# Gates and branch products computed with tokens on the partitions, and latents scaled by 1/rms before they are transposed

## The chip, the cores and the metric

One core of a Trainium2 chip runs the whole program. Its engines are TensorE (PE, matrix products; PEld is its loading of the stationary operand), VectorE (DVE), ScalarE (ACT), GpSimd (POOL) and SyncE (SP, which issues the weight transfers). The metric is the device time of one execution in microseconds.

## The reference

A trunk of two layers works on 256 tokens of width 1024, all in float32. Each layer is a gated feed-forward block, a mixer and a second feed-forward block. The change lies in the mixer:

```python
h = rms_norm(x, mix_norm[l])
rg_x, rg_g, sb_q, sb_k, sb_v, c_q, c_kv, k_r, gate_logits = split(h @ w_in[l])
y_a = rg_lru(conv(rg_x)) * gelu(rg_g)                 # recurrence
y_b = stick_breaking_attention(sb_q, sb_k, sb_v)      # 8 heads
y_c = mla_branch(c_q, c_kv, k_r, ...)                 # rms_norm(c_q) @ w_uq, rms_norm(c_kv) @ w_ukv, softmax attention
g_a, g_b, g_c = split(sigmoid(gate_logits))
merged = g_a * (y_a @ w_branch_a) + g_b * (y_b @ w_branch_b) + g_c * (y_c @ w_branch_c)
x = x + merged @ w_out[l]
```

The three gates and the three branch products are 1024 x 1024 products for 256 tokens each. `c_q` and `c_kv` (the latents) are 256 wide.

## The kernel before

**Products in three parts.** Each float32 weight is split into a high and a low part: ACT casts a piece of 1024 columns to `hi`, and DVE subtracts to get `lo`. Activations are split in the same way into `r` tiles that hold high and low part side by side. A product is hi x hi + hi x lo + lo x hi.

**Two kinds of group.** A *feature group* makes 256 output features on the partitions and keeps tokens along the columns. For each 128 rows of the input (a k-step) the weight is the stationary operand: two matmuls of 512 columns with `hi` (the activations' two parts at once), then two of 256 columns with `lo`. In a view these read `acc<-r,hi` and `acc<-r,lo`. The two halves of the 512 columns are added afterwards (`features`: an ACT copy and a DVE add), and a column of 1/rms values has to be spread over the partitions first (`broadcast`, a matmul against a constant) to be multiplied in. A *token group* makes 512 output features along the columns with the tokens on the partitions. For each k-step the activations are stationary, and each half of the tokens takes three matmuls of 512 columns: `acc<-hi,r`, `acc<-lo,r`, `acc<-hi,r`. Its result is complete, and 1/rms is one number per partition.

**Order.** `MIX_ORDER` is a list, written by hand, of the mixer's groups; `v0` is a token group, `q0` a feature group, and so on. The weights lie in memory in that order and arrive in it. All other work of a layer (the recurrence, two attentions, norms, transposes) is written as tasks. After each k-step `Tasks.tick` lets the tasks add instructions to the engines' queues, by a planner that keeps its own estimates of when each engine is free (`Clock`, `Op.cost`, `fits`). The order is fixed when the program is built; each engine then runs its queue strictly in order. Where a group needs a result that a task has not yet issued, `tasks.drain` issues the rest of that task at once.

**Buffers.** PSUM has two `acc` buffers of two banks, used in turn by groups, and four `side` banks for tasks and for short or last groups (`small_banks`). The dependencies are tracked by tile, so an instruction that reads one half of a tile waits for the writer of the other half too.

**The steps that the change touches.** `latents` copies a latent out of PSUM, transposes it with four 128 x 128 transposes (`side<-cst,f`), splits it with `hilo`, and only then squares it, gets 1/rms on POOL and broadcasts it (`side<-f,cst`), for `head_T` to multiply in. `gate` scales a group and takes a tanh; `branch` multiplies a group by its gate and adds it to `merged`; the third branch of a feature block also splits the sum into an `r` tile, `mT`, which the groups `out0` to `out3` read. `rg_chain` is the recurrence, pair by pair of blocks (four pairs): it splits the block weights and the input into `r` tiles and multiplies them (`side<-r,r`). In the profile all recorded instructions have line L201, so they are told apart by their tiles.

Of the kernel before, what the change touches and what calls it, by code (L numbers as in the profile page):

```python
# [14 lines left out]
NT = S // 128  # L15
# [15 lines left out]
MIX_ORDER = tuple((x.rstrip("0123"), int(x[-1])) for x in """  # L31
v0 k0 rgx0 rgx1 k1 q0 q1 cq0 q2 q3 k2 rgx2 v1 k3 rgx3 rgg0 rgg1 rgg2 rgg3
gb0 uq0 gb1 uq1 gb2 uq2 gb3 uq3 uqr0 brb0 brb1 ckv0 brb2 brb3 ga0 ukv0 ga1 ukv1 uv0 ga2 ukv2
ga3 ukv3 bra0 bra1 uv1 gc0 bra2 gc1 gc2 gc3 brc0 brc1 brc2 brc3 bra3 out0 out1 out2 out3
""".split())
# [3 lines left out]
    "rgx": ("in", 0, KD), "rgg": ("in", 1024, KD), "q": ("in", 2048, KD), "k": ("in", 3072, KD), "cq": ("in", C_C, KD),  # L39
    "ga": ("in", C_G, KD), "gb": ("in", C_G + 1024, KD), "gc": ("in", C_G + 2048, KD),  # L40
    "uq": ("uq", 0, 2), "ukv": ("ukv", 0, 2), "bra": ("bra", 0, KD), "brb": ("brb", 0, KD), "brc": ("brc", 0, KD), "out": ("out", 0, KD),
    "dn1": ("dn1", 0, KF), "dn2": ("dn2", 0, KF),
}
TOKENS = {"last": ("dn2", 0, KF), "v": ("in", 4096, KD), "uqr": ("uq", 1024, 2), "uv": ("ukv", 1024, 2)}


def group_stream(what, n):

    if what == "ckv":
        for k in range(0, 9, 3):  # L50
            yield ("ckv0", "in", k, C_C + 256)
            yield ("ckv1", "in", k, C_C + 256)
    elif what in TOKENS:
# [284 lines left out]
def trunk(tc, xT_in, pos_in, w_in, rgw_in, fin_in, const_in, out):  # L338
# [4 lines left out]
    with ctx:  # L343
# [167 lines left out]
        def feature_group(kts, evac, last=0):  # L511
# [19 lines left out]
            return finish(evac, a, tasks.LAST if last else None)  # L531

        def plain_group(c, xg, evac, norm):

# [55 lines left out]
        def scaled(a, src, key, extra=None, plain=False):  # L590

            if plain:
# [6 lines left out]
                return f  # L599
            f = yield from features(a)  # L600
            while key not in src:
                yield 1
# [76 lines left out]

        def broadcast(b, r, dst, key, start=False):  # L680
# [4 lines left out]
            pe.matmul(b[:, 256:512], neg_one, d[:, 0:256], start=start, stop=True, skip_group_check=True)  # L685
# [131 lines left out]

        def gen_scaled(a, scales):

            o = []  # L820
            for t in range(NT):
                f = yield from FT.take()
                if t == 0:
# [118 lines left out]
        def head_T(mx, key, p, r, extra=None):  # L942

            def run(a):
                f = yield from scaled(a, mx["nm"] if r == "rb" else mx, r, extra)
                yield
                mx[key][p] = f
# [65 lines left out]
        def latents(mx, i):  # L1013
            def run(a):
# [16 lines left out]
                yield  # L1031
                side.give(b)
                mx["cT"][i] = hl
                yield
                junk = yield from FT.take()
                for t in range(NT):
                    act.activation(out=junk[:, 0:256], in_=cs_[t], func=AF.Square, accum_out=mx["ssc"][:, i, t:t + 1])
                yield
                FT.give(junk, c)
                rsqrt_mean(mx["rc"][:, i], mx["ssc"][:, i], 256)  # L1040
                yield
# [20 lines left out]
        def q_rope(mx):  # L1062
            def run(a):
                qs = yield from gen_scaled(a, mx["rq"])
                yield
# [125 lines left out]
        def mix(nm, ntasks, nxt, l):  # L1191
# [6 lines left out]
            mx["rc"] = pool.tile([128, 2, NT], F32, name=f"rc{l}")  # L1198
            mx["rq"] = [mx["rc"][:, 0, t:t + 1] for t in range(NT)]
            mx["rkv"] = [mx["rc"][:, 1, t:t + 1] for t in range(NT)]  # L1200
            mx["sm"] = pool.tile([128, 3, HEADS, NT], F32, name=f"sm{l}")
# [41 lines left out]
            def gate(b, n):  # L1243
                def sigmoid(f):

                    act.activation(out=f, in_=f, func=AF.Tanh, scale=0.5)
                    yield
                    sig[b, n] = f

                def run(a):  # L1250
                    f = yield from scaled(a, mx["nm"], "rb")
                    yield
                    tasks.spawn(sigmoid(f))
                return run

            def branch(i, b, n):

                def run(a):
                    f = yield from FT.take()
                    hl = (yield from RT.take()) if i == 2 else None  # L1260
                    while (b, n) not in sig or (i and n not in merged):
                        yield 1
                    s = sig.pop((b, n))
                    m = merged[n] if i else None
                    for c, ap in parts(a):
                        fc, sc = two(f)[:, c], two(s)[:, c]
                        act.copy(fc, ap[:, :, 256:512])
                        dve.tensor_tensor(fc, ap[:, :, 0:256], fc, op=ALU.add)
                        if type(a) is not list:
                            yield  # L1270
                            give_banks(a)
                        dve.scalar_tensor_tensor(out=fc, in0=sc, scalar=1.0, in1=fc, op0=ALU.add, op1=ALU.mult)
                        if i:
                            mc = two(m)[:, c]
                            dve.tensor_tensor(mc, mc, fc, op=ALU.add)
                        if i == 2:
                            act.copy(hl[:, c, 0], mc)
                            dve.tensor_tensor(hl[:, c, 1], mc, hl[:, c, 0].bitcast(F32), op=ALU.subtract)
                    yield
                    if type(a) is list:  # L1280
                        give_banks(a)
                    FT.give(s)
                    if i == 0:
                        merged[n] = f
                        return
                    FT.give(f)
                    if i == 2:
                        FT.give(m)
                        mT[n] = hl
                return run  # L1290
# [16 lines left out]
            for g in MIX_ORDER:  # L1307
# [5 lines left out]
                elif what == "uq":  # L1313
                    feature_group(Latent(0), head_T(mx, "qn", n, "rbq"))
                elif what == "uqr":
                    token_group(Latent(0), q_rope(mx))
                elif what == "ukv":
                    feature_group(Latent(1), head_T(mx, "kn", n, "rbkv"))
                elif what == "uv":
                    token_group(Latent(1), head_v(mx, "v_ml", n, mx["rkv"]))  # L1320
                elif what == "rgx":
# [7 lines left out]
                elif what in ys:  # L1329
                    mtask[n] = feature_group(Pairs(mx[ys[what]], lambda p: work[what][p:p + 1] if what == "bra" else work[what], KD), branch(turn[g], what[2], n), last=4 if g == branches[-1] else 0)  # L1330
                elif what == "out":
                    out_tasks.append(feature_group(Pairs(mT, lambda p: [mtask[p]], KD), lambda a, n=n: update_x(n, a, 0.5, nxt), last=4 if n == 3 else 0))
                else:
                    feature_group(kts, gate(what[1], n))
                if what in ys and n == 3:
                    RT.give(*mx[ys[what]].values())
# [3 lines left out]
                if g == last_of("rgx", "rgg", "q", "k", "v", "cq", "ckv", "ga", "gb", "gc"):  # L1340
                    RT.give(*nm["xT"].values())
            FT.give(nm["rb tile"], mx["rbq tile"], mx["rbkv tile"])
            FT.give(mx["kr"])
# [174 lines left out]
```

## Time and profile before

| | us |
|---|---|
| median of 3 runs | 1461.55 (1461.19 to 1462.02) |
| the profiled execution's own time | 1463.23 |
| its span, first to last instruction | 1461.4 |
| PE busy in the span | 1442.5 |
| DVE busy | 1108.8 |
| ACT busy | 888.8 |

The span is the part of the execution that the trace covers; 1.8 us lie around it. A busy time is the time in which an engine had at least one instruction under way. Matmuls overlap each other in the pipeline, so the cost of one is the distance from its start to the next one's start, not its duration.

### The profile page before, as it was taken

To read this page: it belongs to the slowest core of one execution; us is meant where nothing else is said; L and a number is where in the kernel's file an instruction comes from. 1 tells how busy PE (TensorE), PEld (TensorE's weight loads), DVE (VectorE), ACT (ScalarE), POOL (GpSimd) and SP (SyncE) were. 2 spreads that over 40 slices of the span, in tenths; PEclk is the share of its full clock that TensorE was granted. 3 is DMA by queue.
4 is the path that set the end of the run, shared out by engine and by line. 5 is a ranking of instruction groups with operands and counts; after the bars stand their busy time and mean duration, and the time that the engine had idled before them with its cause. 6 is when DMAs were issued, how large, how long until landed. Compare 5 with 4: busy or idle time off the path is not lost.

```text
span 1461.4 us, 20833 instructions
## 1 busy us (share of the span) xinstructions
PE 1442.5 (99%) x8276; PEld 1261.0 (86%) x8276; DVE 1108.8 (76%) x1548; ACT 888.8 (61%) x1365; POOL 144.5 (10%) x118
## 2 busy tenths in 40 slices
PE   8999999999999999999999999999999999999998
PEld 7888889888888888888888888898888888888886
DVE  5887567689987788876677776676989877877853
ACT  4665446888665556555455554479885656566543
POOL 2000001123410000000000000111323000100001
PEclk9999999999999999999999999999999999999999
DMA  6555554444543455455545455544444434545452
GB/s 244 201 185 192 200 179 163 170 151 147 197 148 145 171 179 194 179 200 178 198 173 201 177 198 184 200 159 155 141 171 174 173 138 166 199 175 201 176 199 87
DMA packets 37506, 258.17 MB, mean 177 GB/s; under 512 B 4256, under 2 KB 4640, under 8 KB 6816
## 3 DMA queue, kind: packets, MB, share of 16 engines
q1 hardware_dynamic: 35856, 253.16, 48.0%
q0 software_dynamic: 832, 2.62, 0.6%
q8 instruction: 65, 1.06, 0.3%
q10 hardware_dynamic: 720, 1.05, 0.2%
q14 instruction: 33, 0.27, 0.1%
HBM read 255.77 MB, written 1.05 MB: 176 GB/s over the span
## 4 chain that ended last, share of the span: by engine, by line
PE 90%; DVE 7%; issue 1%; ACT 1%; DMA 0%; ACTq 0%; POOLq 0%; POOL 0%; DVEq 0%
PE acc L201 76%; PE side L201 14%; DVE f L201 3%; DVE lo L201 3%; DVE r L201 1%; DMA x<-xT 0%; ACT f L201 0%; ACT hi L201 0%; ACT r L201 0%; ACTq L396 0%; POOLq L1514 0%; POOL rms L201 0%; DVE rms L201 0%; DVEq L201 0%
## 5 line engine op out<-in xcount | busy, mean ns | idle before, releaser
L201 PE MATMUL acc<-r,hi 128*128 128x512 f32 x3116 | 1000.3, 402 | 0.0
L201 DVE TENSOR_TENSOR lo<-raw,hi 128x1024 fp32r<-128x1024 f32 (+1 forms) x478 | 591.4, 1239 | 231.4 <-ACT hi L201 230.2
L201 PEld LDWEIGHTS acc<-r,lo 128*128 128x128 f32 x3116 | 585.2, 188 | 137.7
L201 PE MATMUL acc<-r,lo 128*128 128x256 f32 x3116 | 613.4, 278 | 0.0
L201 ACT CAST hi<-raw 128x1024 fp32r<-128x1024 f32 (+1 forms) x478 | 496.9, 1045 | 128.8 <-PE acc L201 91.9
L201 PEld LDWEIGHTS acc<-r,hi 128*128 128x128 f32 x3116 | 481.5, 189 | 5.0
L201 POOL TENSOR_TENSOR f<-f,f 128x512 f32<-128x512 f32 (+1 forms) x51 | 90.9, 1787 | 1043.3 <-ACT f L201 959.9
L201 ACT COPY f<-acc 128x512 f32<-128x512 f32 x164 | 96.0, 585 | 121.4 <-PE acc L201 121.2
L201 ACT ACTIVATE f<-f 128x256 f32<-128x256 f32 (+3 forms) x190 | 94.9, 502 | 85.6 <-DVE f L201 84.4
L201 DVE TENSOR_TENSOR f<-acc,f 128x512 f32<-128x512 f32 x166 | 113.9, 686 | 41.6 <-ACT f L201 41.2
L201 DVE TENSOR_TENSOR f<-f,f 128x512 f32<-128x512 f32 (+1 forms) x177 | 125.0, 706 | 7.8 <-ACT f L201 1.6
L201 ACT CAST r<-f 128x256 fp32r<-128x256 f32 (+2 forms) x130 | 58.7, 456 | 63.4 <-DVE f L201 59.7
L201 PE MATMUL acc<-hi,r 128*128 128x512 f32 (+2 forms) x344 | 96.9, 358 | 0.0
L201 PE MATMUL side<-r,hi 128*128 128x512 f32 x260 | 84.5, 396 | 0.0
L201 PE MATMUL side<-f,f 128*128 128x256 f32 (+1 forms) x320 | 71.7, 328 | 0.0
L201 PEld LDWEIGHTS acc<-hi,r 128*128 128x128 f32 x344 | 61.6, 189 | 8.3
L201 DVE TENSOR_TENSOR r<-f,r 128x256 fp32r<-128x256 f32 (+2 forms) x130 | 64.7, 502 | 1.9 <-ACT r L201 1.9
L201 PE MATMUL acc<-lo,r 128*128 128x512 f32 (+2 forms) x172 | 61.0, 355 | 0.0
L201 PE MATMUL side<-r,lo 128*128 128x256 f32 x260 | 60.5, 279 | 0.0
L201 PEld LDWEIGHTS side<-r,hi 128*128 128x128 f32 x260 | 45.6, 188 | 7.5
L201 PEld LDWEIGHTS side<-r,lo 128*128 128x128 f32 x260 | 47.0, 188 | 4.0
L201 PEld LDWEIGHTS side<-f,f 128*128 128x128 f32 x320 | 46.0, 191 | 0.5
(95 smaller groups left out, 839.1 us busy)
## 6 DMA issues: line engine op xcount, KB each, us to landing
raw<-w SPq DMA_DIRECT2D x239, 1024.0 KB, 4.8
f<-rgw POOLq DMA_DIRECT2D x8, 256.0 KB, 3.6
raw<-w SPq DMA_DIRECT2D x4, 256.0 KB, 5.7
out<-f SPq DMA_DIRECT2D x4, 256.0 KB, 2.2
x<-xT ACTq DMA_DIRECT2D x3, 256.0 KB, 6.9
f<-fin POOLq DMA_DIRECT2D x2, 256.0 KB, 3.4
cst<-const SPq DMA_DIRECT2D x1, 336.0 KB, 8.3
x<-xT ACTq DMA_DIRECT2D x2, 128.0 KB, 3.8
```

Of the source, the lines that this page charges most:

```text
L201: return self.f(*self.args, **self.kw)
```

## The change

The gates and branches become token groups: 12 groups of 256 features become 6 of 512 for each of the two kinds in a layer. `gate` now copies both token halves out with ACT, times 1/rms; `branch` multiplies straight out of PSUM. `merged` has tokens on the partitions, so after the last branch it is transposed (16 transposes a layer) before it is split into `mT`. The groups `out0` and `out1` become one `outs0`, which goes through the first half of the k-steps for both and then through the second half. The latents are squared first, multiplied by 1/rms on DVE and then transposed, so that four broadcasts go, and the heads need no scaling. `MIX_ORDER` is rewritten.

```diff
-v0 k0 rgx0 rgx1 k1 q0 q1 cq0 q2 q3 k2 rgx2 v1 k3 rgx3 rgg0 rgg1 rgg2 rgg3
-gb0 uq0 gb1 uq1 gb2 uq2 gb3 uq3 uqr0 brb0 brb1 ckv0 brb2 brb3 ga0 ukv0 ga1 ukv1 uv0 ga2 ukv2
-ga3 ukv3 bra0 bra1 uv1 gc0 bra2 gc1 gc2 gc3 brc0 brc1 brc2 brc3 bra3 out0 out1 out2 out3
+v0 k0 rgx0 rgx1 k1 q0 q1 cq0 q2 q3 k2 rgx2 v1 k3 rgx3 rgg0 rgg1 uq0 rgg2 uq1 rgg3 uq2
+gb0 uq3 gb1 uqr0 brb0 ckv0 brb1 ukv0 ga0 ukv1 uv0 ga1 ukv2 bra0 ukv3 uv1 gc0 gc1 bra1 brc0 brc1
+outs0 out2 out3
...
+        def feature_pair(kts, evacs):
+            nk = len(kts)
+            a = [bank() for _ in range(2)]
+            it = iter(kts)
+            for f in range(2):
+                half = [next(it) for _ in range(nk // 2)]
+                for n in range(2):
+                    for i, (h, _, hl) in enumerate(half, f * nk // 2):
...
@@ latents
+                junk = yield from FT.take()
+                for t in range(NT):
+                    act.activation(out=junk[:, 0:256], in_=cs_[t], func=AF.Square, accum_out=mx["ssc"][:, i, t:t + 1])
+                yield
+                FT.give(junk)
+                rsqrt_mean(mx["rc"][:, i], mx["ssc"][:, i], 256)
+                for t in range(NT):
+                    dve.tensor_scalar(cs_[t], cs_[t], mx["rc"][:, i, t:t + 1], None, op0=ALU.mult)
                 yield
                 b = yield from transpose_pair(cs_, 0)
...
-                b = yield from side.take()
-                yield from broadcast(b, mx["rc"][:, i], mx, ("rbq", "rbkv")[i], start=True)
@@ gate
-                    f = yield from scaled(a, mx["nm"], "rb")
+                    for t in range(NT):
+                        f = yield from FT.take()
+                        act.activation(out=f, in_=bank_of(a, t), func=AF.Copy, scale=mx["rcol"][t])
...
@@ branch
-                        act.copy(fc, ap[:, :, 256:512])
-                        dve.tensor_tensor(fc, ap[:, :, 0:256], fc, op=ALU.add)
...
-                        dve.scalar_tensor_tensor(out=fc, in0=sc, scalar=1.0, in1=fc, op0=ALU.add, op1=ALU.mult)
+                    for t, f in enumerate(fs):
+                        dve.scalar_tensor_tensor(out=f, in0=f, scalar=1.0, in1=bank_of(a, t), op0=ALU.add, op1=ALU.mult)
+                        if i:
+                            dve.tensor_tensor(merged[n][t], merged[n][t], f, op=ALU.add)
...
+                    if i == 2:
+                        for q in range(2):
+                            x = yield from transpose_pair(merged[n], q * 256)
+                            hl = yield from RT.take()
+                            hilo(x, hl)
```

**How the order moves.** Three places are shown. Tile names carry buffer numbers here; on PE the names behind the arrow are the moving and then the stationary operand.

*First place: the gates of branch b in layer 0, where `rg_chain` multiplies pairs 2 and 3.* Before, PE's queue at the start of `gb0` reads as follows (`r8`, `r7` belong to pair 2, `r3`, `r13` to pair 3).

```order
L201 MATMUL side2_88<-r3_93,r13_103 128x256 x4
L201 MATMUL acc0_84<-r15_105,hi_2946 128x512 x2
L201 MATMUL acc0_84<-r15_105,lo_2947 128x256 x2
L201 MATMUL side3_89<-r8_98,r7_97 128x256 x4
L201 MATMUL acc0_84<-r15_105,hi_2946 128x512 x2
L201 MATMUL acc0_84<-r15_105,lo_2947 128x256 x2
```

DVE's queue before, from the low part `lo_2947`, which the feature group reads just then, to the last split of pair 3.

```order
L201 TENSOR_TENSOR lo_2947<-raw_2811,hi_2946 128x1024
L201 TENSOR_TENSOR f17_123<-acc0_84,f17_123 128x512
L201 TENSOR_TENSOR f17_123<-f17_123,f2_108 128x512
L201 SCALAR_TENSOR_TENSOR f26_132<-f24_130,f25_131 128x256
L201 TENSOR_TENSOR r8_98<-f14_120,r8_98 128x512
L201 TENSOR_TENSOR lo_2980<-raw_2811,hi_2979 128x1024
L201 TENSOR_TENSOR r13_103<-f15_121,r13_103 128x512
L201 TENSOR_TENSOR r3_93<-f16_122,r3_93 128x512
```

In the changed order PE's queue in the sixth of `gb0`'s eight k-steps (pair 3 is now `r6`, `r13`).

```order
L208 MATMUL acc0_84<-hi_3058,r1_91 128x512
L208 MATMUL acc0_84<-lo_3059,r1_91 128x512
L208 MATMUL acc0_84<-hi_3058,r1_91 128x512 x2
L208 MATMUL acc0_84<-lo_3059,r1_91 128x512
L208 MATMUL acc0_84<-hi_3058,r1_91 128x512
L208 MATMUL side2_88<-r6_96,r13_103 128x256 x4
L208 MATMUL acc0_84<-hi_3091,r1_91 128x512
L208 MATMUL acc0_84<-lo_3092,r1_91 128x512
```

And DVE's queue from three rows ahead of that split.

```order
L208 SCALAR_TENSOR_TENSOR r11_101<-f8_114,r11_101 128x2x256
L208 TENSOR_TENSOR f34_140<-side3_89,f34_140 128x256
L208 TENSOR_TENSOR lo_3092<-raw_2966,hi_3091 128x1024
L208 TENSOR_TENSOR r6_96<-f28_134,r6_96 128x512
L208 TENSOR_TENSOR lo_3109<-raw_2966,hi_3108 128x1024
```

The four matmuls of pair 3 stood in front of a weight part (`lo_2947`) that DVE makes seven rows ahead of pair 3's own split; now their split comes one row behind the weight part that the next matmuls read (`lo_3092`). Pair 2's matmuls moved back into `rgg0`, where their split stands five rows behind the stream's weight part instead of seven.

*Second place: behind `ckv0`, the second latent.* Before, PE's queue in the feature group `brb3`: the broadcast (`f16`, the constant as stationary) ahead of the group's last k-step.

```order
L201 MATMUL acc0_84<-r4_94,hi_3536 128x512 x2
L201 MATMUL acc0_84<-r4_94,lo_3537 128x256 x2
L201 MATMUL side1_87<-f16_122,cst_72 128x256
L201 MATMUL acc0_84<-r4_94,hi_3536 128x512 x2
L201 MATMUL acc0_84<-r4_94,lo_3537 128x256 x2
```

In the changed order PE's queue in the token group `brb1`, between the halves of its sixth k-step: the transposes of the scaled latent (`f31`) and three of the queries' rope part.

```order
L208 MATMUL acc0_84<-hi_3451,r4_94 128x512 x2
L208 MATMUL acc0_84<-lo_3452,r4_94 128x512
L208 MATMUL acc0_84<-hi_3451,r4_94 128x512
L208 MATMUL side3_89<-cst_72,f31_137 128x128 x4
L208 MATMUL side2_88<-cst_72,f35_141 128x128
L208 MATMUL side2_88<-cst_72,f15_121 128x128
L208 MATMUL side2_88<-cst_72,f35_141 128x128
L208 MATMUL acc0_84<-hi_3451,r4_94 128x512
L208 MATMUL acc0_84<-lo_3452,r4_94 128x512
```

The broadcast is gone. The transposes that start the latent's split now wait for the squares, 1/rms and the scaling, and `ukv0`, which reads the split, starts at the end of this group.

*Third place: from the last branch group to the output groups.* Before, PE's queue from the last k-steps of `bra3` into `out0`; the `r` tiles that `out0` reads in its first six k-steps (`r15`, `r0`, `r1`) come from earlier branch groups.

```order
L201 MATMUL side3_89<-r4_94,hi_4793 128x512 x2
L201 MATMUL side3_89<-r10_100,hi_4793 128x512 x2
L201 MATMUL side3_89<-r4_94,lo_4794 128x256 x2
L201 MATMUL side3_89<-r10_100,lo_4794 128x256 x2
L201 MATMUL acc1_85<-r15_105,hi_4817 128x512 x2
L201 MATMUL acc1_85<-r15_105,lo_4818 128x256 x2
L201 MATMUL acc1_85<-r15_105,hi_4817 128x512 x2
L201 MATMUL acc1_85<-r15_105,lo_4818 128x256 x2
```

In the changed order PE's queue at the middle of `outs0`: `f16` and `f27` hold the two token halves of `merged` from `brc1`, `r7` is the first tile split from them.

```order
L208 MATMUL acc1_85<-r4_94,lo_4386 128x256 x2
L208 MATMUL side0_86<-cst_72,f16_122 128x128
L208 MATMUL acc1_85<-r4_94,hi_4385 128x512 x2
L208 MATMUL acc1_85<-r4_94,lo_4386 128x256 x2
L208 MATMUL side0_86<-cst_72,f27_133 128x128
L208 MATMUL side0_86<-cst_72,f16_122 128x128
L208 MATMUL side0_86<-cst_72,f27_133 128x128
L208 MATMUL side3_89<-cst_72,f16_122 128x128
L208 MATMUL side3_89<-cst_72,f27_133 128x128
L208 MATMUL side3_89<-cst_72,f16_122 128x128
L208 MATMUL side3_89<-cst_72,f27_133 128x128
L208 MATMUL acc0_84<-r7_97,hi_4422 128x512 x2
```

DVE's queue at the same place, from the low part of `r4` (the tile that the first half of `outs0` reads in its third and fourth k-step) on; `f4` and `f33` are `brc1` times its gate.

```order
L208 TENSOR_TENSOR r4_94<-side3_89,r4_94 128x2x256
L208 TENSOR_TENSOR lo_4423<-raw_4336,hi_4422 128x1024
L208 SCALAR_TENSOR_TENSOR f4_110<-f4_110,side2_88 128x512
L208 TENSOR_TENSOR f16_122<-f16_122,f4_110 128x512
L208 SCALAR_TENSOR_TENSOR f33_139<-f33_139,side1_87 128x512
L208 TENSOR_TENSOR f27_133<-f27_133,f33_139 128x512
L208 TENSOR_TENSOR lo_4447<-raw_4336,hi_4446 128x1024
L208 TENSOR_TENSOR r7_97<-side0_86,r7_97 128x2x256
L208 TENSOR_TENSOR r10_100<-side3_89,r10_100 128x2x256
```

The last branch's sum stands on DVE behind the split of `r4` and one weight part, and PE's transposes of it stand directly ahead of the matmuls that read their result.

## Rows read from the trace of the kernel before

**Rows 1.** The page: busy time, then TensorE's granted clock, then the ending chain.
```profile
PE 1442.5 (99%) x8276; PEld 1261.0 (86%) x8276; DVE 1108.8 (76%) x1548; ACT 888.8 (61%) x1365; POOL 144.5 (10%) x118
...
PEclk9999999999999999999999999999999999999999
...
PE 90%; DVE 7%; issue 1%; ACT 1%; DMA 0%; ACTq 0%; POOLq 0%; POOL 0%; DVEq 0%
```

**Rows 2.** The waits of PE over the whole span.
```profile
PE side L201 <- DVE r L201: 4.7, 4, 1.5
...
PE side L201 <- DVE f L201: 2.4, 4, 1.0
```

**Rows 3.** PE's timeline in a feature group: start, duration, operation, out<-moving,stationary.
```profile
211.28 0.63 PE L201 MATMUL acc<-r,hi 128*128 128x512 f32 x2
211.75 0.40 PE L201 MATMUL acc<-r,lo 128*128 128x256 f32 x2
...
214.07 0.62 PE L201 MATMUL acc<-r,hi 128*128 128x512 f32 x2
```

**Rows 4.** PE's timeline in a token group.
```profile
200.14 0.62 PE L201 MATMUL acc<-hi,r 128*128 128x512 f32 x2
...
205.58 0.61 PE L201 MATMUL acc<-hi,r 128*128 128x512 f32 x2
```

**Rows 5.** PE's timeline around four transposes of the first latents.
```profile
257.03 0.60 PE L201 MATMUL side<-cst,f 128*128 128x128 f32 x4
...
257.94 0.40 PE L201 MATMUL acc<-r,lo 128*128 128x256 f32 x2
```

**Rows 6.** PE's timeline around a broadcast that nothing holds up.
```profile
210.16 0.59 PE L201 MATMUL side<-f,cst 128*128 128x256 f32 x2
...
211.05 0.40 PE L201 MATMUL acc<-r,lo 128*128 128x256 f32 x2
```

**Rows 7.** PE's timeline around the broadcast of the second latents' 1/rms.
```profile
402.29 0.40 PE L201 MATMUL acc<-r,lo 128*128 128x256 f32 x2
403.73 0.70 PE L201 MATMUL side<-f,cst 128*128 128x256 f32 x2 [1.04 <-DVE f L201]
...
404.72 0.40 PE L201 MATMUL acc<-r,lo 128*128 128x256 f32 x2
```

**Rows 8.** PE's timeline at the transposes of the queries' rope part.
```profile
394.74 0.27 PE L201 MATMUL side<-cst,f 128*128 128x128 f32 x1
395.17 0.55 PE L201 MATMUL side<-cst,f 128*128 128x128 f32 x3 [0.16 <-DVE f L201]
```

**Rows 9.** PE's timeline at the recurrence blocks' matmuls of pairs 2 and 3.
```profile
335.23 0.36 PE L201 MATMUL side<-r,r 128*128 128x256 f32 x1
336.47 0.39 PE L201 MATMUL side<-r,r 128*128 128x256 f32 x1 [0.88 <-DVE r L201]
...
338.57 0.28 PE L201 MATMUL side<-r,r 128*128 128x256 f32 x1
340.31 0.62 PE L201 MATMUL side<-r,r 128*128 128x256 f32 x3 [1.46 <-DVE r L201]
```

**Rows 10.** DVE's timeline just before and in those waits.
```profile
336.34 1.63 DVE L201 TENSOR_TENSOR lo<-raw,hi 128x1024 fp32r<-128x1024 f32 x1
337.89 2.36 DVE L201 TENSOR_TENSOR r<-f,r 128x512 fp32r<-128x512 f32 x2
```

**Rows 11.** GpSimd's timeline in the same stretch.
```profile
336.98 2.13 POOL L201 TENSOR_TENSOR f<-f,f 128x512 f32<-128x512 f32 x1
```

**Rows 12.** ScalarE by form: the high half of a transposed block.
```profile
L201 ACT CAST r<-side 128x512 fp32r<-128x512 f32 x16 | 9.4, 586 | 17.3 <-PE side L201 17.2
```

**Rows 13.** VectorE by form: count, busy time, mean ns of one.
```profile
L201 DVE TENSOR_TENSOR lo<-raw,hi 128x1024 fp32r<-128x1024 f32 x474 | 588.3, 1242 | 229.7 <-ACT hi L201 228.4
...
L201 DVE SCALAR_TENSOR_TENSOR f<-f,f 128x512 f32<-128x512 f32 x46 | 32.6, 716 | 1.0
...
L201 DVE TENSOR_TENSOR r<-side,r 128x512 fp32r<-128x512 f32 x16 | 10.9, 683 | 5.1 <-ACT r L201 5.1
```

More of the change, by code (lines that the diff above doesn't have):

```diff
@@ L52, in group_stream @@
             yield ("ckv1", "in", k, C_C + 256)
+    elif what == "outs":
+        for h in range(2):
+            for n in range(2):
+                for k in range(KD // 2 * h, KD // 2 * (h + 1), 2):
+                    yield ("two", "out", k, 256 * n)
     elif what in TOKENS:
@@ L531, in feature_group @@
             return finish(evac, a, tasks.LAST if last else None)
+        def feature_pair(kts, evacs):
[4 more added lines that the diff above has]
+                half = [next(it) for _ in range(nk // 2)]
+                for n in range(2):
+                    for i, (h, _, hl) in enumerate(half, f * nk // 2):
+                        if i % 2 == 0:
+                            wh, wl = next_sub()
+                        cs_ = [slice((i % 2) * 256 + b * 128, (i % 2) * 256 + (b + 1) * 128) for b in range(2)]
+                        for b, c in enumerate(cs_):
+                            pe.matmul(a[n][:, b], wh[:, c], hl, start=i == 0, stop=False, skip_group_check=True)
+                        for b, c in enumerate(cs_):
+                            pe.matmul(a[n][:, b, 0:256], wl[:, c], h, start=False, stop=i == nk - 1, skip_group_check=True)
+                        tasks.tick()
+            return [finish(e, x) for e, x in zip(evacs, a)]
         def plain_group(c, xg, evac, norm):
@@ L600, in scaled @@
             f = yield from features(a)
+            if key is None:
+                return f
             while key not in src:
@@ L678, in squares, with broadcast @@
             yield from broadcast(b, nm["r"], nm, "rb")
-        def broadcast(b, r, dst, key, start=False):
+        def broadcast(b, r, dst, key):
             d = yield from FT.take()
@@ L944, in run @@
             def run(a):
-                f = yield from scaled(a, mx["nm"] if r == "rb" else mx, r, extra)
+                f = yield from scaled(a, mx["nm"], r, extra)
                 yield
@@ L1032, in run @@
                 side.give(b)
+                FT.give(c)
                 mx["cT"][i] = hl
[L1034 to L1041, printed above, removed]
-                b = yield from side.take()
-                yield from broadcast(b, mx["rc"][:, i], mx, ("rbq", "rbkv")[i], start=True)
                 if i == 1:
@@ L1063, in run @@
             def run(a):
-                qs = yield from gen_scaled(a, mx["rq"])
+                qs = yield from gen_scaled(a)
                 yield
@@ new lines, in run @@
+                    yield
+                    give_banks(a)
+                    if i == 0:
+                        merged[n] = fs
+                        return
+                    FT.give(*fs)
+                    if i == 2:
[3 more added lines that the diff above has]
+                            hilo(x, hl)
+                            yield
+                            side.give(x)
+                            mT[2 * n + q] = hl
+                        FT.give(*merged[n])
@@ L1329, in mix @@
                 elif what in ys:
-                    mtask[n] = feature_group(Pairs(mx[ys[what]], lambda p: work[what][p:p + 1] if what == "bra" else work[what], KD), branch(turn[g], what[2], n), last=4 if g == branches[-1] else 0)
+                    mtask[n] = token_group(Pairs(mx[ys[what]], lambda p: work[what][p:p + 1] if what == "bra" else work[what], KD), branch(turn[g], what[2], n), last=4 if g == branches[-1] else 0)
+                elif what == "outs":
+                    out_tasks += feature_pair(Pairs(mT, lambda p: [mtask[p // 2]], KD), [lambda a, n=n: update_x(n, a, 0.5, nxt) for n in range(2)])
                 elif what == "out":
-                    out_tasks.append(feature_group(Pairs(mT, lambda p: [mtask[p]], KD), lambda a, n=n: update_x(n, a, 0.5, nxt), last=4 if n == 3 else 0))
+                    out_tasks.append(feature_group(Pairs(mT, lambda p: [mtask[p // 2]], KD), lambda a, n=n: update_x(n, a, 0.5, nxt), last=4 if n == 3 else 0))
                 else:
-                    feature_group(kts, gate(what[1], n))
-                if what in ys and n == 3:
+                    token_group(kts, gate(what[1], n))
+                if what in ys and n == 1:
                     RT.give(*mx[ys[what]].values())
@@ L1341, in mix @@
                     RT.give(*nm["xT"].values())
-            FT.give(nm["rb tile"], mx["rbq tile"], mx["rbkv tile"])
+            FT.give(nm["rb tile"])
             FT.give(mx["kr"])
```

62 lines of the change are left out of this document (22 added, 40 removed).

## Prediction

> **What bounds the kernel now.** [...] In four k-steps of a feature group the starts move by 214.07 - 211.28 = 2.79 us, so a k-step (two matmuls of 512 columns, two of 256) costs 0.698, of which the two of 512 take 0.47 and the two of 256 the other 0.23 [rows 3]. Eight triples of a token group take 205.58 - 200.14 = 5.44 us, 0.680 each [rows 4]. Last, the view of PE's waits: they are few, and those for DVE with a side result stand out, 4.7 and 2.4 us [rows 2]. The timeline places them, one set in each layer: the matmuls of `rg_chain` [rows 9], the broadcast behind `ckv0` [rows 7], the rope transposes [rows 8].
>
> **The change, part by part.**
>
> *Gates and branches as token groups.* A layer has 12 + 12 feature groups of eight k-steps, each for 256 features: 192 k-steps, 384 in two layers. As token groups these are 12 groups of eight k-steps with two triples each, 384 triples in two layers. The columns are the same (1536 in a step and in a triple); what differs is four matmuls against three. By the rows the feature steps cost 384 x 0.698 = 268.0 us and the triples 384 x 0.680 = 261.1. **Minus 6.9 us.**
>
> [...]
>
> *Transposes and broadcasts.* The merged sums need 16 transposes a layer, 32 in all. Four transposes and the two matmuls of 512 behind them take 257.94 - 257.03 = 0.91 us; less 0.47, that is 0.11 for one [rows 5]. **Plus 3.5 us.** Four broadcasts go. One without a wait takes, with the two of 512 behind it, 211.05 - 210.16 = 0.89, so 0.42 alone [rows 6]. **Minus 1.7 us.**
>
> *The wait at the broadcast behind `ckv0`.* From one pair of 256 to the next lie 404.72 - 402.29 = 2.43 us; less the pair itself (0.23) and 0.89 for an undisturbed broadcast with its pair, 1.3 is waiting [rows 7]. It goes in both layers, **minus 2.6 us**. What is late next is the latent itself: squares, 1/rms on POOL and scaling now come ahead of its transposes, which stand after five of `brb1`'s eight k-steps, 5 x 2 x 0.680 = 6.8 us behind `ckv0` (the rope transposes add some). The split of the latent has the last three k-steps, 4.1 us, before `ukv0` reads it, and dependencies go by tile, so both halves must be done. No row shows this chain in its new order. Its bounds are nothing and the wait that the same chain causes now, 1.3 in a layer; behind PE at that point stand all later groups. I take 0.4, nearer to nothing, since the DVE instruction that PE needs here stands six rows behind the weight part that the stream reads, where that of the broadcast stood eight behind: **plus 0.8 us**. `cq0` has two feature groups and most of a third between itself and its transposes, and costs nothing.
>
> *The rope transposes.* The second of them starts 0.43 behind the first instead of 0.11: 0.32 of waiting [rows 8]. Now two k-steps of a token group stand between the first, written by POOL, and the second, written by DVE. Bounds nothing and 0.32 in a layer; I take it as gone, **minus 0.6 us**.
>
> *The waits of `rg_chain`.* Pair 2's second matmul starts 336.47 - 335.23 = 1.24 behind its first, where 0.12 (half a pair of 256) would do: 1.1 of waiting. Pair 3's starts 340.31 - 338.57 = 1.74 behind: 1.6 [rows 9]. DVE is late there: a weight split takes 1.63 instead of its mean of 1.24 [rows 10, 13], and two splits of the recurrence 2.36 together, both beside a POOL operation of 2.13 [rows 11]. In the order before, these matmuls need a DVE instruction seven rows behind the weight part that the stream reads at that moment, so DVE's lead over the stream is not enough. In the new order pair 3 needs one that is one row behind, with a token group whose gate is copied out by ACT alone, and pair 2 one that is five rows behind, in a denser place. For pair 3 the bounds are 0 and 1.6 in a layer, and I take it as gone: minus 3.2. For pair 2 they are 0 and 1.1, and I take half: minus 1.1. **Minus 4.3 us** together.
>
> *The passage from `brc1` to `outs0`.* Before, `out0` reads three tiles of earlier groups for six k-steps (4.2 us) while the last one is made, and the waits show nothing there. Now, let T be the end of `brc1`'s last matmul. PE does four transposes (0.44). ACT casts (0.59) and DVE subtracts (0.68) to make `r4` [rows 12, 13]; with 0.16 for the tail of a transpose (0.27 long where the next comes after 0.11 [rows 5, 8]) and 0.06 at each of three handovers (DVE ends at 337.89 + 2.36 = 340.25, PE starts at 340.31 [rows 9, 10]) it is ready at T + 2.05. PE reads `r9` until T + 0.44 + 1.40 = T + 1.84, so it waits 0.2. The last branch's own sums stand behind `r4` on DVE: a weight part (1.24), then four operations of about 0.72 each [rows 13], so `f27` is there at about T + 6.1. PE comes to the transposes of `f27` after the first half of `outs0` (eight k-steps, 5.6 us), the short wait and one transpose, at T + 0.44 + 5.6 + 0.2 + 0.11 = T + 6.35, so it does not wait there. Three transposes end at T + 6.7; tail, cast, subtraction and handovers take 1.6 more, to T + 8.3, while PE has only the other four transposes to do, until T + 7.15. It waits 1.1. Together 1.3 in a layer, **plus 2.6 us**. The bounds: the second wait has a floor of 1.1, since the transposes stand directly ahead of their readers however early DVE is; above, one weight part more on DVE, 1.24, at both waits. That is 1.1 to 3.8 in a layer.
>
> *What costs nothing.* `gate` leaves ACT two copies for 512 features where ACT and DVE had two copies, two additions and two multiplications; `branch` drops ACT copies and DVE additions. All of it lies beside PE, which two `acc` buffers keep going: a token group lasts 10.9 us and its buffer is next needed a group later. If that cover went, a copy of about 0.7 would show in each of 24 groups. The weights keep their number and size, so the transfers stay.
>
> **The sum.** - 6.9 + 3.5 - 1.7 - 2.6 + 0.8 - 0.6 - 4.3 + 2.6 = - 9.2 us. The profiled execution took 1463.23 us with a span of 1461.4, so 1.8 lie around it; the median of the runs is 1.7 below it. The terms are differences, so I take them from the median: 1461.55 - 9.2 = 1452.4 us.
>
> **The rivals.**
>
> *New waits take the place of the removed ones.* The order is fixed by a planner whose estimates led PE into the waits of [rows 7, 9]; a new order has new such places. For it: the tasks get half as many turns in a token group, since a turn comes once in a k-step, and that is now twice as long. Against it: in the attention and gate stages the waits view shows almost nothing now. If the 2.6, 0.6 and 4.3 all return elsewhere, 1461.55 - 9.2 + 7.5 = 1459.9, within a change that can't be told from none.
>
> *The columns alone set the pace.* If the triples of gates and branches come at 0.698 like the steps, having as many columns, the first term is nothing: 1452.4 + 6.9 = 1459.3. Against it: the triples of [rows 4] are the same instructions. [...]
>
> *Slower: the passage to `outs0` costs more than everything else gives.* Every later group stands behind those two waits. Without them the change gives 11.8 us, 5.9 in a layer, so it decides when PE waits over 5.9 in a layer. That needs DVE to reach `r4` some 4.6 late, nearly four weight parts of 1.24. It would give 1464 or more. Against it: ahead of T, DVE waits for PE's transposes, so it has no arrears.
>
> *The change doesn't do what it says:* the gates' and branches' rows would keep the form `acc<-r,hi`. The built order excludes that.
>
> **How the numbers follow.** The forecast, 1452.4 us, has a chance of 0.70, with its own bounds from 1450.1 (pair 2's wait gone too, minus 1.1; none at the latents, minus 0.8; none at the start of `outs0`, minus 0.4) to 1456.6 (2.5 in a layer at `outs0`, plus 2.4; 1.3 at the latents, plus 1.8). New waits: 0.18. The columns alone: 0.03. Slower: 0.05; the rest, 0.04, lies below 1450. The range that leaves out no more than 2 in 10 takes in the forecast's bounds and the nearer part of the new waits, from 1449 to 1459. A measurement of this kernel can tell about 0.2%, or 2.9 us, from no change: 1458.6 divides. Faster by more than that: the forecast, the part below it and half of the new waits, 0.83. Within it: the other half and the columns alone, 0.12. Slower: 0.05.
>
> **What would show it.** In the trace after, the gates' rows are `acc<-hi,r` triples at 0.680; 32 more transposes of 0.11; no wait at `side<-f,cst` behind the latents; `side<-r,r` waits of pair 3 gone; in each layer one wait of about 1 us in the middle of `outs0`, for the low half of a split, and a short one near its start. The forecast is wrong if PE's waits add up to more than before, or if triples in the middle of branch groups come at 0.70.

## The result and the profile after

The changed kernel takes 1472.03 us (median of 4 runs, 1469.96 to 1472.34), beside it the kernel before 1461.78 (4 runs): ratio 1.0066, interval 1.0049 to 1.0083. It is slower by 10.3 us; the prediction had 9.2 faster, with a range that ends at 1459.

The page of the changed kernel answers to [rows 1]: busy times, TensorE's granted clock, the ending chain.

```profile
PE 1445.7 (98%) x7916; PEld 1244.6 (85%) x7916; DVE 1048.9 (71%) x1452; ACT 873.6 (59%) x1333; POOL 140.1 (10%) x118
...
PEclk9999999999999999999999999999999999999999
...
PE 88%; ACT 4%; DVE 3%; issue 2%; POOL 2%; DMA 1%; ACTq 0%; POOLq 0%
```

DVE, ACT and POOL have less to do than before and PE is still the bound, but its share of the chain has fallen from 90% to 88%. PE's waits (engine, tile and line waited for; us in total, times, the longest) answer to [rows 2]:

```profile
PE side L208 <- DVE f L208: 7.5, 4, 2.1
PE side L208 <- ACT f L208: 3.0, 4, 0.8
PE side L208 <- DVE r L208: 2.2, 4, 0.6
PE acc L208 <- DVE r L208: 1.9, 2, 1.0
```

Each comes twice or four times: the same places in both layers. Before, two such rows held 4.7 and 2.4 us; now four hold 14.6. (Waits for DVE in the first 12 us of the program, 2.8 us in the trace before and 1.4 in this one, are not in these sums: the instructions there are the same.) Triples have the price that was read ahead, as in [rows 4]; PE's timeline in `ga0`, two triples apart, gives (412.58 - 411.22) / 2 = 0.680:

```profile
411.22 0.62 PE L208 MATMUL acc<-hi,r 128*128 128x512 f32 x2
...
412.58 0.62 PE L208 MATMUL acc<-hi,r 128*128 128x512 f32 x2
```

So the rate is right and the waits are not. PE's timeline where the recurrence and the first attention run (columns as in [rows 3]):

```profile
323.87 0.40 PE L208 MATMUL side<-r,hi 128*128 128x512 f32 x1
325.02 0.50 PE L208 MATMUL side<-r,hi 128*128 128x512 f32 x1 [0.76 <-ACT f L208]
...
332.45 0.34 PE L208 MATMUL side<-r,tri_r 128*128 128x384 f32 x1
333.36 0.44 PE L208 MATMUL side<-r,tri_r 128*128 128x384 f32 x1 [0.57 <-DVE r L208]
...
333.78 0.48 PE L208 MATMUL side<-r,hi 128*128 128x512 f32 x1
335.02 0.50 PE L208 MATMUL side<-r,hi 128*128 128x512 f32 x1 [0.76 <-ACT f L208]
...
343.18 0.39 PE L208 MATMUL side<-r,hi 128*128 128x512 f32 x1
345.65 0.47 PE L208 MATMUL side<-r,hi 128*128 128x512 f32 x1 [2.08 <-DVE f L208]
```

`side<-r,hi` here is one of the short groups `uq0`, `uq1`, `uq2` (two k-steps, 1.4 us when nothing holds them up), which use side banks. Each time the first matmul, into the first bank, runs, and the second, with the same activations but into the other bank, waits: 1.15, 1.24 and 2.47 from start to start where 0.23 would do, so 0.92, 1.01 and 2.24 are waiting; with 0.73 at the attention's `side<-r,tri_r` that is 4.9 us in a layer. What holds the last bank is seen on DVE:

```profile
343.23 1.93 DVE L208 TENSOR_TENSOR lo<-raw,hi 128x1024 fp32r<-128x1024 f32 x1 [1.01 <-ACT hi L208]
345.09 0.41 DVE L208 TENSOR_TENSOR f<-side,f 128x256 f32<-128x256 f32 x1
```

The bank is still to be read (`f<-side,f`), and the read stands behind a weight part. By its shape it is the second half of the sum in which `features` reads a short group out, so at `uq2` it is `uq1`'s own result that holds the bank. At `uq0` and `uq1` the reads that end last are ACT's, of the recurrence and of the attention. [rows 9] are gone: the recurrence's matmuls no longer wait. So is the broadcast of [rows 7], but the latent's transposes in `brb1` wait in its place, 401.99 - 399.93 - 0.23 = 1.83 (PE, then GpSimd, then DVE):

```profile
399.93 0.39 PE L208 MATMUL acc<-hi,r 128*128 128x512 f32 x1
401.99 1.13 PE L208 MATMUL side<-cst,f 128*128 128x128 f32 x7 [1.67 <-DVE f L208]
```

```profile
397.65 1.72 POOL L208 TENSOR_TENSOR f<-f,f 128x512 f32<-128x512 f32 x1 [6.36 <-DVE f L208]
399.50 1.01 POOL L208 TENSOR_SCALAR rc<-ssc 128x2 f32<-128x2 f32 x1
400.59 0.72 POOL L208 TENSOR_TENSOR rc<-rc,nhalf 128x2 f32<-128x2 f32 x1
```

```profile
398.50 1.95 DVE L208 TENSOR_TENSOR lo<-raw,hi 128x1024 fp32r<-128x1024 f32 x1 [0.27 <-ACT hi L208]
401.35 0.84 DVE L208 TENSOR_SCALAR f<-f,rc 128x256 f32<-128x256 f32 x2 [0.89 <-POOL rc L208]
```

The two POOL operations and the scalings, all new ahead of the transposes, end just when PE goes on. In the middle of `outs0` PE waits as predicted: the seven transposes start at 533.39 and take 0.77, the next matmul starts at 535.28, so 1.12.

```profile
533.39 0.93 PE L208 MATMUL side<-cst,f 128*128 128x128 f32 x7
535.28 0.72 PE L208 MATMUL acc<-r,hi 128*128 128x512 f32 x2 [0.96 <-DVE r L208]
```

One more, about 0.7 a layer (0.51 of it idle), lies where `uv1` follows directly on `ukv3`, both short groups.

### The profile page after: what moved, and what is told of

Same layout as the page of the kernel before. It is cut to its first block, busy times and chain, and to the rows that moved or that the text cites. A ratio compares the mean times of both kernels' runs of the same rounds, so it can differ in the third digit from the quotient of the medians.

```text
span 1470.5 us, 19993 instructions
## 1 busy us (share of the span) xinstructions
PE 1445.7 (98%) x7916; PEld 1244.6 (85%) x7916; DVE 1048.9 (71%) x1452; ACT 873.6 (59%) x1333; POOL 140.1 (10%) x118
## 4 chain that ended last, share of the span: by engine, by line
PE 88%; ACT 4%; DVE 3%; issue 2%; POOL 2%; DMA 1%; ACTq 0%; POOLq 0%
PE acc L208 73%; PE side L208 15%; ACT f L208 2%; DVE f L208 2%; POOL f L208 1%; ACT hi L208 1%; DVE lo L208 1%; ACT L143 1%; DMA x<-xT 0%; DVE r L208 0%; DMA raw<-w 0%; POOL rc L208 0%; ACT r L208 0%; ACTq L403 0%; POOLq L1540 0%
## 5 line engine op out<-in xcount | busy, mean ns | idle before, releaser
L208 PE MATMUL acc<-r,hi 128*128 128x512 f32 x2380 | 757.2, 399 | 1.9 <-DVE r L208 1.9
L208 PEld LDWEIGHTS acc<-r,lo 128*128 128x128 f32 x2380 | 447.0, 188 | 105.5
L208 PE MATMUL acc<-r,lo 128*128 128x256 f32 x2380 | 468.1, 278 | 0.0
L208 PEld LDWEIGHTS acc<-r,hi 128*128 128x128 f32 x2380 | 364.9, 189 | 4.6 <-DVE r L208 2.8
L208 PE MATMUL acc<-hi,r 128*128 128x512 f32 (+2 forms) x1048 | 340.8, 391 | 0.0
L208 PEld LDWEIGHTS acc<-hi,r 128*128 128x128 f32 x1048 | 194.5, 189 | 35.1
L208 PE MATMUL acc<-lo,r 128*128 128x512 f32 (+2 forms) x524 | 199.1, 380 | 0.0
L208 PEld LDWEIGHTS acc<-lo,r 128*128 128x128 f32 x524 | 99.2, 189 | 16.1 <-DVE lo L208 0.3
L208 DVE TENSOR_TENSOR f<-acc,f 128x512 f32<-128x512 f32 x120 | 82.2, 685 | 33.5 <-ACT f L208 33.4
L208 PE MATMUL side<-hi,r 128*128 128x512 f32 x200 | 64.5, 393 | 1.0 <-DVE r L208 1.0
```

Source lines behind the costliest of these rows:

```text
L208: return self.f(*self.args, **self.kw)
```

## The experiments

**Theory A, the place.** A short group needs two of the four side banks at once. Before it is put on PE's queue, `small_banks` pushes the tasks on until two banks have been handed back on paper; PE then meets banks whose last reader on ACT or DVE has not come yet, or attention matmuls pushed ahead of their operands. Among `rgg1` to `rgg3` the recurrence, the first attention and the short group before hold the banks. The latents' wait is apart from that: the planner puts the transposes where it believes the scaled latent to be ready, and its estimate of the two POOL operations is too small. **Theory B, half as many turns.** Tasks get their turn once in a k-step, and that lasts 1.36 us in a token group instead of 0.70, so all side work comes late, wherever the short groups stand.

*Short groups moved back.* `e1_uq_back`:

```diff
-rgg0 rgg1 uq0 rgg2 uq1 rgg3 uq2
-gb0 uq3 gb1 uqr0 brb0 ckv0 brb1 ukv0 ...
+rgg0 rgg1 rgg2 rgg3 uq0
+gb0 uq1 gb1 uq2 uqr0 brb0 uq3 ckv0 brb1 ukv0 ...
```

> The changed kernel with one thing moved: the short groups uq0, uq1, uq2 stand behind rgg3, between the token groups (uq0 gb0 uq1 gb1 uq2 uqr0 brb0 uq3), where the kernel before had them, instead of among rgg1 to rgg3. Theory A (the place): a short group needs two of the four side banks at once, and among rgg1 to rgg3 the recurrence and the first attention hold them, so PE waits there for ACT and DVE to read a bank out: 0.92 + 0.73 + 1.01 + 2.24 = 4.9 us in a layer. Then these waits go, 9.8 us less, about 1462, or up to 5.5 more than that if the two waits of rg_chain come back. Theory B (half as many turns): a token group gives the tasks a turn only every 1.36 us, so tasks are late wherever the short groups stand; the waits return at the new place and the time stays within 2 us of 1472.

Measured 1468.53 (ratio to before 1.0047, 1.0035 to 1.0060), between the two: over theory A's upper end and under theory B's lower one. PE's timeline shows why: `uq1` and `uq2`, now behind `gb0` and `gb1`, do not wait; `uq0`, still directly behind `rgg3`, does, 1.65; and the latents wait more, 397.58 - 394.48 - 0.23 = 2.87.

```profile
333.17 0.39 PE L208 MATMUL side<-r,hi 128*128 128x512 f32 x1
335.05 0.50 PE L208 MATMUL side<-r,hi 128*128 128x512 f32 x1 [1.49 <-ACT f L208]
```

```profile
394.48 0.39 PE L208 MATMUL acc<-hi,r 128*128 128x512 f32 x1
397.58 1.38 PE L208 MATMUL side<-cst,f 128*128 128x128 f32 x5 [2.71 <-DVE f L208]
```

Behind that wait the granted clock falls to half, 0.50 all through the two microseconds from 398 on. The view of windows has a stretch, its length, the busy times of PE, PEld, DVE, ACT and POOL, and then the granted clock, the DMA share and GB/s:

```profile
394.00:398.00 4.00, 1.29 (x6) 0.72 (x5) 3.11 (x6) 2.62 (x6) 1.24 (x2) 0.90 0.40 115
398.00:400.00 2.00, 2.00 (x8) 1.74 (x8) 2.00 (x4) 0.48 (x1) 1.54 (x1) 0.50 0.91 377
```

*The planner's estimate for POOL.* `e2_pool_cost`, in `Op`:

```diff
             self.cost = 150 + (166 if kw.get("op") == ALU.pow else 2.1) * n
+            if out.tensor.name.startswith("rc"):
+                self.cost = 730 if kw.get("op") == ALU.pow else 1100
```

> The changed kernel, where only the planner's estimate for the two small POOL operations of the latents' 1/rms is raised (154 to 1100 ns and 482 to 730 ns, near what the trace of the changed kernel shows in the second latent: 1007 and 722); the operations are the same. On PE it only moves the four transposes of each latent later. Theory A: the wait of 1.83 us in a layer in brb1 is the planner's doing, which puts the transposes on PE's queue when it believes the scaled latent to be ready; 2.5 to 3.7 us less, 1468.3 to 1469.5. Rival: the chain itself is too long for the room behind it (squares, POOL, two scalings on DVE behind a weight part), so the same wait shows at the new place or at ukv0, and the time stays within 1 us.

Measured 1466.62 (1.0041, 1.0028 to 1.0054): 5.5 us above the kernel before, where the changed kernel is 10.3 above it. That is 4.8 less, but the two intervals overlap, and the two profiled executions differ by 2.3 us before the edit can matter: the first `acc<-r,hi` starts at 24.84 us in the changed kernel and at 22.54 here, behind the same instructions. From there to PE's last matmul this trace is 2.3 us shorter, less than the 3.7 of the wait in two layers. PE's timeline has the latent's four transposes at their new place, two k-steps (four triples) further on, and without a wait:

```profile
401.79 0.39 PE L210 MATMUL acc<-hi,r 128*128 128x512 f32 x1
402.03 0.60 PE L210 MATMUL side<-cst,f 128*128 128x128 f32 x4
```

No instruction was added or dropped, and of the wait only 0.17 a layer is left, at `ukv0`. So the 1.83 us were the planner's placing, not a chain too long for its room; how much of them the time gives back, 2.3 or up to 4.8, is not settled.

*Latents as before.* `e3_latents_undone`, the changed kernel with the old `latents` (its lines in the diff ahead of the prediction, taken back) and the scaling in the heads:

> The changed kernel with the latents as before: transposed and split at once, 1/rms broadcast afterwards (four broadcasts more) and multiplied in by the heads. If the latents' part is about even, as its rows say (wait of 1.83 a layer in brb1 gone, broadcast wait of up to 1.25 a layer and 0.25 to 0.4 for each of four broadcasts back), the time stays within 2 us of the changed kernel. If the latents' part is what makes the change slow, 4 us or more go. In either case the waits at uq0 to uq2 stay.

Measured 1468.64 (1.0050, 1.0037 to 1.0064), 2 to 3 us less than the changed kernel, intervals that overlap. The wait in `brb1` is gone, but the waits among `rgg1` to `rgg3` have taken another form (2.3 and 1.7 at `side<-r,tri_r`), so the difference is not the latents' alone: inconclusive.

*The new place, in the kernel before.* `e4_before_uq_ahead`:

```diff
-rgg0 rgg1 rgg2 rgg3
-gb0 uq0 gb1 uq1 gb2 uq2 gb3 uq3 uqr0 ...
+rgg0 rgg1 uq0 rgg2 uq1 rgg3 uq2
+gb0 uq3 gb1 gb2 gb3 uqr0 ...
```

> The kernel before, all feature groups, with one thing moved: uq0, uq1, uq2 among rgg1 to rgg3, as the changed kernel has them (then gb0 uq3 gb1 gb2 gb3 uqr0). Theory A (the place): waits of about 1 us and more at the second bank of the short groups, as in the changed kernel, 4 to 5 in a layer; the two waits of rg_chain (2.7 in a layer) may go. 1464 to 1471. Theory B (half as many turns): no such waits, as the tasks have their full number of turns; if rg_chain's waits go as well, 1456 to 1462.

Measured 1474.29 (1.0087, 1.0073 to 1.0100), above theory A's range: the kernel before, all feature groups, becomes 13 us slower by the place of short groups alone (`uq3`, now behind `gb0`, moves with the other three). The waits are not at the second bank, as expected, but in PE's timeline directly ahead of `uq0`:

```profile
323.72 0.45 PE L201 MATMUL side<-r,tri_r 128*128 128x384 f32 x1 [2.30 <-ACT r L201]
325.87 0.44 PE L201 MATMUL side<-r,tri_r 128*128 128x384 f32 x1 [1.70 <-DVE r L201]
...
326.37 2.64 PE L201 MATMUL side<-f,f 128*128 128x256 f32 x8
```

The attention's matmuls stand ahead of their operands, as the pushing by `small_banks` would put them. The windows add a cost that the waits view does not hold: the granted clock falls to 0.50 behind these waits.

```profile
321.00:326.00 5.00, 1.00 (x6) 0.55 (x5) 4.78 (x8) 1.41 (x4) 2.57 (x3) 1.00 0.58 210
...
327.00:329.00 2.00, 2.00 (x8) 1.73 (x8) 0.00 (x0) 0.12 (x1) 0.00 (x0) 0.50 0.00 0
...
330.00:332.00 2.00, 2.00 (x14) 1.74 (x13) 1.75 (x3) 1.97 (x3) 0.00 (x0) 1.00 0.00 0
```

There is also a new wait of 1.99 in a layer in `brc0`, for a DVE result. The rg_chain waits are gone here as well, without token groups: they were a matter of order too.

*As many turns as before.* `e6_ticks`, in `token_group`:

```diff
                 for t in range(NT):
                     ...
+                    tasks.tick()
                 held = []
-                tasks.tick()
```

> The changed kernel, where a token group gives the tasks a turn after each of its triples instead of after each k-step, so as many turns as the feature groups gave. Theory A (the place of the short groups and the estimate of the latents' 1/rms): the waits among rgg1 to rgg3, which are feature groups, stay at 4 to 5 us a layer, the latents still wait, and the time is within 4 us of 1472. Theory B (half as many turns): the waits in and behind the token groups go, and the time falls by 5 us or more.

Measured 1474.66 (1.0092, 1.0078 to 1.0106). More turns do not help; PE waits at the same two places, for the latents (the first row) and ahead of `uq0` (the second):

```profile
PE side L208 <- DVE f L208: 5.5, 4, 1.9
PE side L208 <- ACT r L208: 5.0, 2, 2.5
```

Theory B falls.

*All short groups where banks are free.* `e5_short_apart`, nothing but the order:

```diff
-rgg0 rgg1 uq0 rgg2 uq1 rgg3 uq2
-gb0 uq3 gb1 uqr0 brb0 ckv0 brb1 ukv0 ... bra0 ukv3 uv1 gc0 gc1 ...
+rgg0 rgg1 rgg2 rgg3
+gb0 uq0 gb1 uq1 uqr0 brb0 ckv0 uq2 uq3 brb1 ukv0 ... bra0 uv1 ukv3 gc0 gc1 ...
```

> The changed kernel with only the order of its short groups changed: rgg0 to rgg3 run through, uq0 and uq1 stand behind gb0 and gb1, uq2 and uq3 stand behind ckv0 (where the first attention is over and most side banks are free, and where they give the second latent 2.8 us more time before brb1), uv1 stands ahead of ukv3. Nothing is computed differently. Theory A (a short group makes PE wait where other work holds the side banks): the waits of 4.9 us a layer among rgg1 to rgg3 go and none of over 0.5 takes their place, and of the 1.83 a layer in brb1 between nothing and all goes: 9.8 to 13.5 us less than the changed kernel, 1458.5 to 1462, about the kernel before or up to 3 us faster. Theory B (half as many turns make tasks late wherever the short groups stand): other waits take their place as in the run with uq0 behind rgg3, and it stays above 1466.

Measured 1458.23 (11 runs; ratio to before 0.9981, 0.9972 to 0.9989): 13.4 us less than the changed kernel relative to before, the far edge of theory A, and faster than the kernel before by 3.1. PE's waits:

```profile
PE side L208 <- DVE r L208: 2.8, 4, 1.1
PE acc L208 <- DVE r L208: 1.9, 2, 1.0
...
PE side L208 <- DVE f L208: 0.7, 3, 0.3
```

No short group and no latent waits for more than 0.3 any longer; for the latents, `uq2` and `uq3` give the time. Left are 1.3 in a layer at `side<-r,tri_r` in `gb0` and the 1.1 in `outs0`.

*The last two short groups.* `e7_short_apart_gc` has `uv1 gc0 ukv3` for `uv1 ukv3 gc0`.

> The order with the short groups apart, and gc0 between uv1 and ukv3 as well. In the changed kernel uv1 stands directly behind ukv3 and waits 0.67 us a layer for a side bank. If two short groups in a row are what costs there, this gives 1.3 us over the order with uv1 and ukv3 together; if the last attention then ends later, a wait ahead of brc0 takes its place, and it is 1 to 4 us slower.

Measured 1459.86 (0.9994, 0.9985 to 1.0003). Two short groups in a row cost little by themselves (the order before this one has `uv1 ukv3` in a row, with 0.27 idle there); a wait of 0.7 in a layer in `brc0` is new, and the median is 1.6 higher, with intervals that just overlap: the second expectation, as far as the noise lets it be told.

*More cover at the passage.* `e8_outs_three` does the first half of the k-steps for three output groups, on top of `e5_short_apart`:

```diff
-outs0 out2 out3
+outs0 out3
...
-                for n in range(2):
+                for n in range(3):
+                    if len(a) == n:
+                        a.append(small_banks() if len(side.free) < NT else [side.now() for _ in range(NT)])
```

> The order with the short groups apart, and the passage from brc1 to the output groups with more cover: the first half of the k-steps is done for three output groups (the third one on two side banks) before the second half, 8.4 us instead of 5.6. Theory (the wait of 1.13 us a layer in the middle of outs0 is cover that is too short by that much): the wait goes, 2.3 us less than the order with the short groups apart, about 1456. Rival: three results come out of PSUM together, the updates of x and the next norm come later, and PE waits for them at the next feed-forward block, by the two updates of 1.4 us each or more: 0.5 to 6 us slower than that order, 1459 to 1464.

Measured 1468.56 (1.0058, 1.0045 to 1.0071). The wait in `outs0` is gone, and PE waits instead at the start of the next feed-forward block, 0.74 and

```profile
547.25 0.39 PE L208 MATMUL acc<-r,lo 128*128 128x256 f32 x2
550.71 1.22 PE L208 MATMUL acc<-r,hi 128*128 128x512 f32 x2 [3.07 <-DVE r L208]
```

for the normed x: three results leave PSUM together and the last one's norm comes late. The rival held in kind, 4.6 us beyond its upper end; the two matmuls behind the wait last 1.22 instead of 0.62, and the granted clock is down there too (0.64 from 550 to 552 us, 0.51 from 552 to 554).

## Why the prediction was wrong

**The step that failed** is the one that is not there: the change also moved `uq0`, `uq1` and `uq2` among `rgg1` to `rgg3`, and the working gave them no term, though it used the same rows of the order to say where the recurrence's waits go. They cost 4.9 us a layer, 9.8 in all, and e4 shows that the place costs this much or more with feature groups too. That PE waits there for side banks is read from the timelines; that the place does it is shown by e1, e4 and e5. `uv1` behind `ukv3`, equally without a term, cost some 1.3.

**The latents** were given 0.8 with bounds of nothing and 1.3 a layer; they cost 1.83 a layer, 3.7, outside the bounds. The mechanism was named (squares, POOL and scaling ahead of the transposes), but the upper bound was taken from the wait of the same chain at another place. e2 shows that the planner's placing sets it.

**Right in place and size:** the broadcast's wait ([rows 7]), the rope's ([rows 8]) and both of [rows 9] are gone (the whole of pair 2's, not half: 1.1 more than counted), though in e4 [rows 9] go without any token group, so the token groups' part in that is not shown. The passage to `outs0` costs 0.2 and 1.1 a layer, as worked out; e8 takes the second away.

**The sum of the rest.** With these terms set right the prediction's - 9.2 becomes - 9.2 + 9.8 + 1.3 + 2.9 - 1.1 = + 3.7; measured are + 10.3. In e5 it becomes - 9.2 - 0.8 - 1.1 + 2.6 (the wait in `gb0`) = - 8.5; measured are - 3.1. So 6.6 and 5.4 us are missing. In the changed kernel 1.6 of them are the clock, which falls to half behind the wait at `uq2` in the second layer (0.52 from 1071 to 1074 us, last section); the mean granted clock of the profiled execution is 0.998 there and 0.999 in e5. The other 5 or so are missing in either order, so they lie with the steady gain (- 6.9 + 3.5 - 1.7) rather than with the order. One part can be read in e5's timeline behind four transposes:

```profile
392.75 0.63 PE L208 MATMUL acc<-hi,r 128*128 128x512 f32 x2
...
393.45 0.63 PE L208 MATMUL acc<-hi,r 128*128 128x512 f32 x2
...
394.14 0.63 PE L208 MATMUL acc<-hi,r 128*128 128x512 f32 x2
...
394.83 0.62 PE L208 MATMUL acc<-hi,r 128*128 128x512 f32 x2
...
395.51 0.62 PE L208 MATMUL acc<-hi,r 128*128 128x512 f32 x2
```

The triples come at 0.70, 0.69, 0.69 and only then at 0.68: for a few steps behind side work they have the price of a k-step, and branch groups are full of side work. Over the whole trace of e5, a triple directly behind side work takes 0.785 from start to start (median of 112) and the next one 0.691 (118); a k-step of the kernel before takes 0.785 directly behind side work as well (209), and the next is back at 0.696. So the first triple gains nothing and the second a third of the 0.018; with some 100 more of each than before that is, as an estimate, 3 us of the 6.9. The forecast priced the whole term from a stretch without side work; its own sign of being wrong, triples at 0.70 in the middle of branch groups, is there for these few. The last 2 us or so stay open in either order.

**The rivals.** "New waits take the place of the removed ones" was the right one in kind, at 0.18. Its price was wrong: it let the removed 7.5 us return, but new waits have no reason to equal old ones. Per layer 4.3 us went (1.1 + 1.6 + 1.3 + 0.3) and 8.5 came (4.9 + 1.83 + 0.67 + 1.1). "The columns alone" was not it, at 0.680 for undisturbed triples, though directly behind side work it holds (0.785 for triple and step). The passage to `outs0`, the rival on the slower side, did not decide.

## What to carry to other kernels

Where an order is rewritten, list every group that changes its neighbours and ask of each what it takes at its start (here two of four PSUM banks) and who holds that at the new place; a group that nobody mentioned cost more than all that the change was about. A gain of half a per cent from denser matmuls is smaller than what two or three waits of an in-order queue decide, so the order must be tuned again before such a change can be judged: the same instructions took 1472 and 1458 us. A planner that places work when it believes an operand to be ready turns each estimate that is too small into a wait of the engine that is the bound.

## What the runs showed of the hardware

Two waits of PE in a row (2.30 and 1.70 us, PE busy for 1.00 of 5 us in e4) are followed by some 3 us at or near a granted clock of 0.50 (0.75 from 326 to 327 us, 0.50 to 329, 0.54 to 330), in which eight matmuls of 256 columns take 2.64 us; from 330 us on it is back at 1.00. A single wait can be followed by the same, and need not be. In the changed kernel PE is idle for 2.08 us at `uq2` in the first layer (345.65), and the clock stays at 1.00. Behind the same wait in the second layer, 2.05 us, it is at or near half for some 3 us (0.52 from 1071 to 1074 us), and from the matmul behind the wait to the same triple PE takes 1074.89 - 1070.23 = 4.66 us instead of 348.72 - 345.65 = 3.07:

```profile
348.72 0.62 PE L208 MATMUL acc<-hi,r 128*128 128x512 f32 x2
...
1070.23 0.47 PE L208 MATMUL side<-r,hi 128*128 128x512 f32 x1 [2.05 <-DVE f L208]
...
1074.89 0.62 PE L208 MATMUL acc<-hi,r 128*128 128x512 f32 x2
```

```profile
346.00:349.00 3.00, 3.00 (x17) 2.54 (x16) 2.96 (x6) 1.38 (x4) 0.29 (x1) 1.00 0.41 96
...
1071.00:1074.00 3.00, 3.00 (x10) 2.40 (x9) 2.96 (x6) 1.79 (x4) 0.62 (x2) 0.52 0.51 161
```

In e2 it is the wait in the first layer that the half clock follows (0.50 from 344 to 346 us). So a wait in this stream can cost nearly twice its length (2.05 + 1.59 us here), and one layer does not tell of the other.

A POOL operation on two columns took 1007 ns in the second latent and 193 ns in the first, with the same form. In the second it starts at 399.50, while DVE works on a weight part from 398.50 to 400.45, and ends at 400.51; that part itself takes 1.95 instead of 1.24, and a POOL operation of 1.72 runs over its first 0.87 us. In the first it starts at 258.10, in a stretch of 2.19 us in which DVE is idle. The second layer repeats both: 1.00 with a weight part of 1.95, and 0.19 with DVE idle. So in both layers the two are long where they run beside each other; no run takes one of them away alone, so what makes them long is not shown.
